# Gated delta rule in a two-layer trunk: keys read back and measured ahead of the gates, turned tiles stored in token order, one exponential for a chunk's decay

## The chip, the cores and the metric

The kernel runs on one core of a Trainium2 chip. The metric is the device time of one execution in microseconds, the median of several runs. TensorE (PE) multiplies matrices, VectorE (DVE), ScalarE (ACT) and GpSimd (POOL) work on tiles, and SyncE (SP) issues nearly all DMA transfers, in the order of its own queue. Each engine works through its instructions in the order in which the program holds them.

## The reference

Two layers run over 1024 tokens of width 1024. The change touches only the first layer's mixer. It projects the normed input to a gate branch (u, v), to q, k, v, to z and to two gate values per head, and runs a chunked delta rule on q, k, v:

```python
proj = rms_norm(h, ln_mix_e[i]) @ w_in_e[i]
a_uv, b_qkv, b_z, b_beta, b_a = jnp.split(proj, split_at, axis=-1)
qkv = jax.nn.silu(causal_depthwise_conv(qkv, conv_w))
q = l2_normalize(q) * (B_HEAD_DIM ** -0.5);  k = l2_normalize(k)
beta = jax.nn.sigmoid(beta_logit)
g = -jnp.exp(a_log) * jax.nn.softplus(a_logit + dt_bias)
gc = jnp.cumsum(g, axis=-1)                      # within a chunk
decay = exp(gc[t] - gc[s]) for s <= t, else 0
a = strict_lower((k * beta) @ k.T * decay);  t_mat = a + I
u = solve(t_mat, v * beta);  w = solve(t_mat, k * beta * exp(gc))
# one chunk after the other
v_new = u - w @ state
o = (q * exp(gc)) @ state + (q @ k.T * decay) @ v_new
state = state * exp(gc[-1]) + (k * exp(gc[-1] - gc)).T @ v_new
o = rms_norm(o, out_gain) * silu(z)
```

The layer goes on with an output projection, an MLP and a gated embedding; the second layer has attention instead of the mixer. All that is as it was.

## The kernel before, in words

The kernel keeps float32 accuracy by splitting every operand of a projection in a high and a low part, so that a product is three matmuls (`mm3`). The mixer works on 8 chunks of 128 tokens and 4 heads of 128. Its parts:

- **The fill.** `self.stream([...])` is a list of projections, cut in units. A unit of a `proj_qkv` is one step of the sum for 128 channels and 512 tokens: three matmuls of 512 columns. `pump(n)` emits units until n have been emitted in all. PE always has these units between the delta rule's own small matmuls, which are emitted at high priority and placed among them by a scheduler that writes each engine's order down. 256 units lie ahead of the first step of the recurrence. Weights are cast by ACT (L221) and DVE (L222).
- **A projected tile of q, k or v** is evicted by DVE (L1394), convolved by one ACT pass and three DVE passes (L1398, L1400), passed through tanh (L1402) and a product (L1407), turned in 32 by 32 blocks by DVE (`transpose`, L1408) into a temporary `t` and written to DRAM (`by_token`, L1409). The pool of `t` has four buffers; each tile takes two. `read_tokens` (L1365) brings one chunk back with tokens on the partitions: four transfers, each of 512 pieces of 128 bytes.
- **z** (`proj_z(0)`) also yields the gate values. `gates()` can start only when the last unit of `proj_z(0)` is done. It sums the gates within a chunk by PE (`pg`), turns the sums (`pgt`, L1335), copies them (L1337) and writes them to `g_dram` (L1338). `spatial_weights()` turns the gate branch's weights (`pws`).
- **`ahead(c)`**, for 8 chunks, reads the sums back on all partitions (`du`, L1602) and the chunk's keys as token rows (`kt`), forms the two decay masks `am` and `du` by eight exponentials of 128 columns (L1609) and two selections on POOL (L1610), measures the keys (`inverse_length`, L1582 to L1587), scales them (L1615), multiplies keys by keys on PE (`pkk`, into a PSUM pair shared with `pg`, `pgt`, `pws`), masks the product on DVE (L1629) and writes `am`, `du`, `kt` and the diagonal blocks of `am` to DRAM (L1591, L1632). `du` and `kt` have a place for each of four chunks (slots A0, A3), `am` has two (c6, d0).
- **`solve()`** reads the diagonal blocks of all chunks (L1641), inverts them on DVE in 30 steps of two instructions (L1647, L1648) and writes the result (`solved`, L1651). **`inverse(c)`** reads one chunk of it back (L1689, `inv`), turns it (L1693) and joins the blocks on PE (`py`, `pz`). **`step(c)`** is the recurrence (`pks`, `po`, `pvn`, `pst`), **`prep(c)`** readies its operands and reads v and q by `read_tokens`.

The order of emission is: `pump(96)`, `gates()`, `spatial_weights()`, `pump(104)`, the eight `ahead` spread over FILLA = 40 units, the solve over FILLB = 64, the first inverse over FILLC = 48, then chunk by chunk.

Of the kernel before, what the change touches and what calls it, by code (L numbers as in the profile page):

```python
# [11 lines left out]
F32 = mybir.dt.float32  # L12
# [6 lines left out]
P = 128  # L19
# [12 lines left out]
KA = (6, 5)  # L32
MARKS = ((64, 50), (192, 144), (223, 168))
TAIL = 220
FILLA, FILLB, FILLC = 40, 64, 48
IDLE = 5
FILLS = (24, 24, 24, 24, 28, 28, 28, 28)

# [76 lines left out]
class Trunk:  # L115
# [1141 lines left out]
    def even_mix(self, first, rows_of_rest, rest_of_x, w_in, ws, bs, conv, a_log, dt_bias, v_gain, o_gain, masks, w_out, gain_next, h_dram):  # L1257
# [81 lines left out]
            nc.vector.tensor_scalar(flat(nsum), pg[:, 0], -1.0, None, ALU.mult)  # L1339

        def spatial_weights():
            wsr = self.tmp().rearrange("p (g t) -> p g t", g=G)
            nc.sync.dma_start(wsr, ws.rearrange("g t s -> t g s"))
# [14 lines left out]
        def read_tokens(i, c, out):  # L1358

            hf, n = c // 4, c % 4  # L1360
            assert all((i, hf, m) in made for m in range(G))
            for j in range(4):
                z = slice(32 * j, 32 * j + 32)
                src = by_token[i, hf].rearrange("(a c) t -> c a t", c=32)[:, :, n * P + 32 * j : n * P + 32 * j + 32]
                nc.sync.dma_start(out[z].rearrange("c h (i r) -> c h i r", r=32), src.rearrange("c (h i) r -> c h i r", i=4))  # L1365

        def proj_qkv(i, j, hfs):

            def units(w):
                for hf in hfs:  # L1370
                    if (i, hf) not in by_token:
                        by_token[i, hf] = self.dp.tile([G * P, HT], F32, name=self.nm("by_token"))
                        if i < 2:
                            home(i, hf)

                    first = (i, hf, j) == (1, 0, 0)
                    pss = [self.mm_ps() for _ in range(2)] if first else []
                    for k, ml in itertools.product(range(KT), range(2)) if first else ():
                        self.mm3(pss[ml], w.at(k, slice(ml * P, (ml + 1) * P)), hs_first[k], k == 0, k == KT - 1)
                        if k < KT - 1:  # L1380
                            yield None
                    for ml in range(2):
                        m = i * 4 + j * 2 + ml
                        ps = pss[ml] if first else self.mm_ps()
# [12 lines left out]
                        y = self.tmp()  # L1397
                        nc.scalar.activation(y, cx[:, 3:], AF.Copy, scale=conv[:, 3, m : m + 1])  # L1398
                        for tap in range(3):
                            nc.vector.scalar_tensor_tensor(y, cx[:, tap : tap + HT], conv[:, tap, m : m + 1], y, ALU.mult, ALU.add)  # L1400
                        th = self.tmp()
                        nc.scalar.activation(th, y, AF.Tanh, scale=0.5)  # L1402
                        if i < 2:
                            y, y2 = qkv[i, hf][:, m % 4], y
                        else:
                            y2 = y
                        nc.vector.scalar_tensor_tensor(y, th, 1.0, y2, ALU.add, ALU.mult)  # L1407
                        nc.vector.transpose(th, y)  # L1408
                        nc.sync.dma_start(by_token[i, hf][(m % 4) * P : (m % 4 + 1) * P], th)  # L1409
                        made.add((i, hf, m % 4))  # L1410
                        yield None

# [168 lines left out]
        def inverse_length(pt, name, sq):  # L1581
# [4 lines left out]
            rn = self.sp.tile([P, G], F32, tag=name, name=self.nm(name), bufs=3)  # L1586
            nc.gpsimd.tensor_tensor(rn, l2, self.mhalf[:, 0:G], ALU.pow)  # L1587
            return rn

# [3 lines left out]
        def fetch(c, i, t):  # L1593
            nc.sync.dma_start(flat(t), spill[c, i])
            return t

        def ahead(c):

            if c == 0:
                early.extend(self.slot(t, [P, 4, HT], F32, "early") for t in ("A0", "A3"))  # L1600
            du, kt = (e[:, c % 4].rearrange("p (h t) -> p h t", h=G) for e in early)
            nc.sync.dma_start(flat(du), g_dram[G * c : G * c + G].rearrange("h t -> (h t)").partition_broadcast(P))  # L1602
            read_tokens(1, c, kt)
            yield
            yield
            am = self.slot(("c6", "d0")[c % 2], [P, G, P], F32, "dec")
            for e, own, other in ((am, gsum, 1), (du, nsum, -1)):
                for h in range(G):
                    nc.scalar.activation(e[:, h], du[:, h], AF.Exp, scale=-float(other), bias=own[:, c, h : h + 1])  # L1609
                nc.gpsimd.affine_select(e, e, pattern=[[0, G], [-other, P]], base=0, channel_multiplier=other, compare_op=ALU.is_gt if other > 0 else ALU.is_ge, fill=0.0)  # L1610
            keep(c, 1, du)

            k = part(1, c)
            rk = inverse_length(kt, "rk", self.slot(f"c{4 + c % 2}", [P, G, HD], F32, "sq"))
            nc.vector.tensor_tensor(kt, kt, bc(dec[:, c], HD), ALU.mult)  # L1615
# [12 lines left out]
            for h in range(G):  # L1628
                nc.vector.scalar_tensor_tensor(am[:, h], pp[:, h], sc[:, h : h + 1], am[:, h], ALU.mult, ALU.mult)  # L1629
# [21 lines left out]
            nc.sync.dma_start(solved, flat(x))  # L1651


        mid, ch, early = {}, {}, []

        def prep(c):
            kt = fetch(c, 2, self.slot(f"c{c % 2}", [P, G, HD], F32, "kt"))
# [129 lines left out]
        def mixing():  # L1787
# [15 lines left out]
        states = [state]  # L1803

        fill = itertools.chain(self.stream([
            proj_qkv(1, 0, (0,)), proj_qkv(2, 0, (0,)), proj_qkv(1, 1, (0, 1)), proj_z(0),
            proj_qkv(1, 0, (1,)), proj_qkv(2, 1, (0, 1)),
            proj_uv(1, 0), proj_uv(1, 1), proj_qkv(0, 0, (0,)), proj_qkv(0, 1, (0, 1)),
            proj_z(1), proj_qkv(0, 0, (1,)), proj_qkv(2, 0, (1,)), proj_uv(0, 0), proj_uv(0, 1)], first), mixing())
        closed = []  # L1810
# [12 lines left out]

        pump(2)
        self.wide = ("mm", "sc")
        rows_of_rest()
        for t, c in ((U, 0), (V, P), (mk, 2 * P)):
            nc.sync.dma_start(t, masks[:, c : c + t.shape[1]])
# [3 lines left out]
        nc.vector.tensor_scalar(og, og, 0.5, None, ALU.mult)  # L1832
        for _ in rest_of_x:
            pass
        pump(96)
        gates()
        spatial_weights()
        pump(104)


        def run(g, slot=True):
# [29 lines left out]
        self.pe.start(LAG)  # L1871
        solver = solve()
        systems = [ahead(c) for c in range(NC)]
        for i, n in enumerate(share(FILLA, NC + 3)):
            for j in range(min(i, NC - 1), max(0, i - 3) - 1, -1):
                run(systems[j], False)
            self.pe.slot()
            pump(done + n)
# [152 lines left out]
```

## Time and profile before

| | |
|---|---|
| median of 3 runs | 2528.28 us (2523.44 to 2531.18) |
| the profiled execution | 2529.31 us, its span 2527.6 us |
| PE busy | 2480.6 us, 98% of the span |
| DVE, ACT, POOL busy | 1867.0 us (74%), 1289.1 us (51%), 316.5 us (13%) |
| DMA | 457.76 MB, 59.9% of 16 engines; 239652 of 549876 packets under 512 bytes |

The span is cut in windows and chains by the profile; PE is busy nearly always, so a reader looks for the few stretches in which it is not. The mixer ahead of the recurrence lies in about the first 217 us.

### The profile page before, as it was taken

How to read it: one execution, taken by the hardware profiler on the slowest of the kernel's cores; microseconds unless marked ns; L12 is line 12 of the kernel's file. 1: busy time of each engine (PE TensorE's matmuls, PEld its weight loads, DVE VectorE, ACT ScalarE, POOL GpSimd, SP SyncE). 2: the span in 40 equal slices, each digit the busy share in tenths (PEclk: the TensorE clock that was granted, in tenths of full speed). 3: DMA queues.
4: the chain of work that ended last, by engine and by line, in shares of the span. 5: the costliest groups of instructions: out<-in, count | busy, mean ns of one | idle time of the engine just before them, and what ended most of it. 6: DMA issues, size and time to landing. Idle time of an engine off the chain costs nothing.

```text
span 2527.6 us, 39880 instructions
## 1 busy us (share of the span) xinstructions
PE 2480.6 (98%) x13599; PEld 2113.7 (84%) x13599; DVE 1867.0 (74%) x3611; ACT 1289.1 (51%) x2584; POOL 316.5 (13%) x280
## 2 busy tenths in 40 slices
PE   9979999999999999999999999999999999999999
PEld 7878898888888887888899999987788888878877
DVE  7777777687667779656568888885886677787586
ACT  6553444465455444454356766664655455445442
POOL 0220242000000000000234443341000000000000
PEclk9989999999999999999999999999999999999999
DMA  7584564547555855653347776799375558655651
GB/s 256 167 221 125 134 170 151 168 132 250 176 176 200 298 177 185 192 173 118 111 108 166 160 165 160 172 241 289 129 232 188 177 187 282 211 188 186 194 174 59
DMA packets 549876, 457.76 MB, mean 181 GB/s; under 512 B 239652, under 2 KB 412712, under 8 KB 549672
## 3 DMA queue, kind: packets, MB, share of 16 engines
q1 hardware_dynamic: 549656, 455.21, 59.9%
q8 instruction: 107, 1.75, 0.3%
q14 instruction: 97, 0.79, 0.1%
q10 hardware_dynamic: 16, 0.00, 0.0%
HBM read 320.86 MB, written 134.23 MB: 180 GB/s over the span
## 4 chain that ended last, share of the span: by engine, by line
PE 87%; DVE 4%; DMA 4%; SPq 2%; issue 1%; ACT 1%; POOL 0%; DVEq 0%; ACTq 0%; POOLq 0%
PE mm L76 77%; PE po L76 3%; PE qk L76 2%; PE aux L76 2%; SPq L1365 1%; PE tr L79 1%; DVE w L222 1%; DMA raw<-in_w_ple_gate_dram 1%; DMA aT<-a_dram 0%; DMA a_dram<-lg 0%; PE pgm L76 0%; DVE t L1400 0%; DVE acc L282 0%; DMA by_token<-t 0%; SPq L1632 0%
## 5 line engine op out<-in xcount | busy, mean ns | idle before, releaser
L76 PE MATMUL mm<-g,w 128*128 128x512 f32 x2592 | 603.8, 394 | 1.4 <-DVE acc L282 0.9
L221 ACT CAST w<-raw 128x512 fp32r<-128x512 f32 x598 | 364.7, 617 | 459.2 <-PE mm L76 376.0
L76 PEld LDWEIGHTS mm<-g,w 128*128 128x128 f32 x2592 | 485.9, 188 | 116.9 <-ACT w L221 1.3
L76 PE MATMUL mm<-hi,w 128*128 128x512 f32 x1728 | 555.4, 397 | 0.3 <-ACT hi L1248 0.3
L76 PE MATMUL mm<-w,hi 128*128 128x256 f32 (+2 forms) x2528 | 505.7, 296 | 3.3 <-ACT w L221 3.3
L222 DVE TENSOR_TENSOR w<-raw,w 128x512 fp32r<-128x512 f32 x510 | 353.2, 699 | 184.7 <-ACT w L221 178.7
L76 PEld LDWEIGHTS mm<-w,hi 128*128 128x128 f32 x2528 | 402.9, 190 | 17.6 <-ACT w L221 3.5
L76 PEld LDWEIGHTS mm<-hi,w 128*128 128x128 f32 x1728 | 325.8, 189 | 74.6 <-ACT hi L1248 0.7
L76 PE MATMUL mm<-w,lo 128*128 128x256 f32 (+2 forms) x1264 | 370.2, 294 | 0.0
L76 PE MATMUL mm<-lo,w 128*128 128x512 f32 x864 | 341.9, 396 | 0.9 <-DVE lo L1249 0.9
L76 PE MATMUL mm<-t,w 128*128 128x512 f32 x1152 | 270.8, 394 | 1.2 <-ACT w L221 1.2
L76 PEld LDWEIGHTS mm<-t,w 128*128 128x128 f32 x1152 | 216.2, 188 | 52.7 <-ACT w L221 1.6
L76 PEld LDWEIGHTS mm<-w,lo 128*128 128x128 f32 x1264 | 239.6, 190 | 6.1
L76 PEld LDWEIGHTS mm<-lo,w 128*128 128x128 f32 x864 | 163.4, 189 | 37.3 <-DVE lo L1249 1.4
L222 DVE TENSOR_TENSOR g<-graw,g 128x512 fp32r<-128x512 f32 x216 | 147.4, 686 | 10.6 <-DMA gd<-g 9.8
L221 ACT CAST g<-graw 128x512 fp32r<-128x512 f32 x216 | 132.7, 617 | 33.4 <-PE mm L76 10.8
L258 POOL TENSOR_TENSOR r<-ms,mhalf 128x4 f32<-128x4 f32 x12 | 13.3, 1108 | 1006.9 <-DVE ms L256 979.2
L1030 ACT ACTIVATE lg<-lg,nm 128x128 f32<-128x128 f32 (+7 forms) x128 | 99.2, 775 | 76.3 <-DVE nm L1027 75.5
L222 POOL TENSOR_TENSOR w<-raw,w 128x512 fp32r<-128x512 f32 (+1 forms) x88 | 114.9, 1326 | 142.7 <-ACT w L221 94.0
L348 ACT ACTIVATE g<-g 128x512 f32<-128x512 f32 x96 | 60.5, 632 | 120.5 <-DVE g L282 113.4
L1027 DVE CUSTOM_DVE_ANT_0 lg<-qk,al 128x512 f32<-128x512 f32 (+3 forms) x128 | 74.7, 587 | 27.6 <-PE qk L76 22.3
L76 PE MATMUL mm<-ohi,w 128*128 128x512 f32 x256 | 87.3, 406 | 1.4 <-DVE t L1207 1.4
(332 smaller groups left out, 3538.3 us busy)
## 6 DMA issues: line engine op xcount, KB each, us to landing
raw<-in_w_mlp_dram SPq DMA_DIRECT2D x352, 256.0 KB, 3.1
graw<-gd SPq DMA_DIRECT2D x224, 256.0 KB, 3.0
gd<-g SPq DMA_DIRECT2D x192, 256.0 KB, 3.2
raw<-in_w_ple_gate_dram SPq DMA_DIRECT2D x76, 256.0 KB, 3.2
acc<-h_dram SPq DMA_DIRECT2D x64, 256.0 KB, 4.4
keep<-in_w_mlp_dram SPq DMA_DIRECT2D x64, 256.0 KB, 4.9
raw<-in_w_in_e_dram SPq DMA_DIRECT2D x60, 256.0 KB, 3.9
h_dram<-acc SPq DMA_DIRECT2D x48, 256.0 KB, 2.3
```

Of the source, the lines that this page charges most:

```text
L76: self._next(self.engine.matmul(*a, **k))
L79: self._next(self.engine.transpose(*a, **k))
L221: self.nc.scalar.copy(hi, src)
L222: (lo_engine or self.nc.vector).tensor_tensor(lo, src, f32(hi), ALU.subtract)
L258: nc.gpsimd.tensor_tensor(r, ms, self.mhalf[:, 0:4], ALU.pow)
L348: nc.scalar.activation(g, src, AF.Relu)
L1027: nc.vector.tensor_tensor_reduce(out=lg[:, k0:k1], in0=ps[:, : k1 - k0], in1=al[:, u0 + k0 : u0 + k1], scale=-1.0, scalar=3.0e38 if c == 0 ...
L1030: nc.scalar.activation(lg[:, :n], lg[:, :n], AF.Exp, bias=nm[:, r, nch - 1 : nch], scale=-1.0, accum_out=me.sums[:, b, r : r + 1])
L1365: nc.sync.dma_start(out[z].rearrange("c h (i r) -> c h i r", r=32), src.rearrange("c (h i) r -> c h i r", i=4))
```

## The change

It has six parts.

1. The projections of keys for the second half of the tokens go ahead of `proj_z(0)`, so that all keys are projected before z. The gates then come after 112 units, not 96.
2. A turned tile is written in token order: four transfers of 32 partitions with 512 pieces of 128 bytes each (L1406). A chunk is read back by one transfer of whole rows (L1360).
3. A new generator `lengths(c)` reads and measures the keys of every chunk during the units of z, ahead of the gates. All 8 key tiles now have a place of their own (A0, A3).
4. `du` moves to two slots (c2, c3). POOL subtracts the sums from it once (L1610), and each mask is then one exponential of 512 columns (L1613).
5. The gate branch's weights are loaded near the start, to a slot of their own.
6. `ahead(c)` has three steps, not four; `pump(120)` precedes it, and FILLA, FILLB, FILLC become 36, 56, 44, so that 256 units still lie ahead of the recurrence.

```diff
-FILLA, FILLB, FILLC = 40, 64, 48
+FILLA, FILLB, FILLC = 36, 56, 44
...
-            for j in range(4):
-                z = slice(32 * j, 32 * j + 32)
-                src = by_token[i, hf].rearrange("(a c) t -> c a t", c=32)[:, :, n * P + 32 * j : n * P + 32 * j + 32]
-                nc.sync.dma_start(out[z].rearrange("c h (i r) -> c h i r", r=32), src.rearrange("c (h i) r -> c h i r", i=4))
+            nc.sync.dma_start(flat(out), by_token[i, hf][n * P : (n + 1) * P])
...
-                        nc.sync.dma_start(by_token[i, hf][(m % 4) * P : (m % 4 + 1) * P], th)
+                        for a in range(4):
+                            f0 = (m % 4) * P + 32 * a
+                            nc.sync.dma_start(by_token[i, hf].rearrange("(t c) f -> c t f", c=32)[:, :, f0 : f0 + 32], th[32 * a : 32 * a + 32].rearrange("c (t r) -> c t r", r=32))
...
+        def lengths(c):
+            if c % 4 == 0:
+                early.append(self.slot(("A0", "A3")[c // 4], [P, 4, HT], F32, "early"))
+            kt = early[c // 4][:, c % 4].rearrange("p (h d) -> p h d", h=G)
             read_tokens(1, c, kt)
             yield
+            rks.append(inverse_length(kt, "rk", self.slot(f"c{4 + c % 2}", [P, G, HD], F32, "sq"), NC))
...
+            du = self.slot(f"c{2 + c % 2}", [P, G, P], F32, "dec")
+            nc.sync.dma_start(flat(du), g_dram[G * c : G * c + G].rearrange("h t -> (h t)").partition_broadcast(P))
+            yield
+            nc.gpsimd.tensor_tensor(du, du, bc(gsum[:, c], P), ALU.subtract)
...
-            for e, own, other in ((am, gsum, 1), (du, nsum, -1)):
-                for h in range(G):
-                    nc.scalar.activation(e[:, h], du[:, h], AF.Exp, scale=-float(other), bias=own[:, c, h : h + 1])
+            for e, other in ((am, 1), (du, -1)):
+                nc.scalar.activation(flat(e), flat(du), AF.Exp, scale=-float(other))
...
-            proj_qkv(1, 0, (0,)), proj_qkv(2, 0, (0,)), proj_qkv(1, 1, (0, 1)), proj_z(0),
-            proj_qkv(1, 0, (1,)), proj_qkv(2, 1, (0, 1)),
+            proj_qkv(1, 0, (0,)), proj_qkv(2, 0, (0,)), proj_qkv(1, 1, (0, 1)), proj_qkv(1, 0, (1,)),
+            proj_z(0), proj_qkv(2, 1, (0, 1)),
...
+        wsr = self.slot("c8", [P, G, P], F32, "wsr")
+        nc.sync.dma_start(wsr, ws.rearrange("g t s -> t g s"))
...
-        pump(96)
+        pump(80)
+        tokens = [lengths(c) for c in range(NC)]
+        for i in range(NC + 1):
+            if i:
+                next(tokens[i - 1])
+            if i < NC:
+                next(tokens[i])
+            pump(done + (i < NC) * 4)
         gates()
         spatial_weights()
-        pump(104)
+        pump(120)
...
-        for i, n in enumerate(share(FILLA, NC + 3)):
-            for j in range(min(i, NC - 1), max(0, i - 3) - 1, -1):
+        for i, n in enumerate(share(FILLA, NC + 2)):
+            for j in range(min(i, NC - 1), max(0, i - 2) - 1, -1):
```

In the lists below, numbers after a name tell buffers of the same name apart, and x4 is four equal instructions. The first place is PE where the gates' sums are turned (`pgt`) and the keys' products begin (`pkk`). Before:

```order
L76 MATMUL mm_1371<-hi_127,w_1099 128x512
L79 MATMUL pgt_1079<-ident,carved_239 32x128
L76 MATMUL mm_1371<-lo_128,w_1099 128x512
L76 MATMUL mm_1371<-hi_127,w_1100 128x512
L76 MATMUL mm_1371<-hi_136,w_1099 128x512
L76 MATMUL mm_1371<-lo_137,w_1099 128x512
L76 MATMUL mm_1371<-hi_136,w_1100 128x512
L79 MATMUL pws_1087<-ident,t_1085 128x128
L76 MATMUL pkk_1280<-qkv_275 128x128 x4
L79 MATMUL pws_1087<-ident,t_1085 128x128 x3
```

and now, where `wsr` holds the gate branch's weights:

```order
L76 MATMUL mm_1434<-hi_554,w_1107 128x512
L79 MATMUL pgt_1277<-ident,carved_239 32x128
L79 MATMUL pws_1283<-ident,wsr_288 128x128 x4
L76 MATMUL pkk_1399<-qkv_275 128x128 x4
L76 MATMUL mm_1434<-hi_605,w_1188 128x512
L76 MATMUL mm_1434<-lo_606,w_1188 128x512
L76 MATMUL mm_1434<-hi_605,w_1189 128x512
```

`pgt` stands 41 matmuls of 512 columns later in PE's order than before. Behind it the second `pkk` comes after 12 matmuls of the fill (15 before) and the third after 9 more (12 before). The first `py` stands 27 rows later than before, nearly all of them matmuls of 512 columns.

The second place is SP's queue from the write of the gates' sums on, where `early_1143` and `dec` hold decays and `dec_1194`, `dec_1254` are `am` of the first two chunks. Before:

```order
L1338 DMA g_dram<-t_1081 32x128
L1602 DMA early_1143<-g_dram 128x512 x4
L1409 DMA by_token_702<-t_1138 128x512
L1632 DMA diag<-dec_1194 32x4x32
L1591 DMA spill<-early_1143 128x512
L1632 DMA diag<-dec_1194 32x4x32 x2
L1591 DMA spill<-early_1143 128x512
L1632 DMA diag<-dec_1194 32x4x32
L1591 DMA spill<-dec_1194 128x512
L1602 DMA early_1143<-g_dram 128x512
```

and now, where `dec_1337`, `dec_1355`, `dec_1383`, `dec_1447` are `du` of chunks 0 to 3 and `dec_1358`, `dec_1386` are `am` of chunks 0 and 1:

```order
L1338 DMA g_dram<-t_1279 32x128
L1608 DMA dec_1337<-g_dram 128x512
L1608 DMA dec_1355<-g_dram 128x512
L1406 DMA by_token_437<-t_1329 32x16x32 x4
L101 DMA raw_2128<-in_w_in_e_dram 128x2x256
L1588 DMA spill<-dec_1337 128x512
L1636 DMA diag<-dec_1358 32x4x32
L1588 DMA spill<-dec_1355 128x512
L1636 DMA diag<-dec_1358 32x4x32 x2
L1608 DMA dec_1383<-g_dram 128x512
L1636 DMA diag<-dec_1358 32x4x32
```

Four reads of the sums stood together; now two do, and the third is queued behind the write of the first chunk's `du`, whose slot it takes. POOL's order has the same pairs: subtractions of chunks 2n and 2n+1, then four selections.

The third place is ACT at the last four chunks, where `dec_1557`, `dec_1596`, `dec_1664` are `am` of chunks 4, 5, 6, `t_1761` and `t_1845` are GELU tiles of the gate branch, and `qkv_2300` is v of the first four chunks. Before (ACT's last exponentials and what followed):

```order
L1609 ACTIVATE early_1143<-early_1143,carved_239 128x128
L1609 ACTIVATE dec_1636<-early_1143,carved_239 128x128 x4
L1609 ACTIVATE early_1143<-early_1143,carved_239 128x128 x4
L1476 ACT_TABLE_LOAD
L1476 ACTIVATE t_1806<-mm_1745,r_217 128x256 x2
```

and now:

```order
L1473 ACTIVATE t_1761<-mm_1648,r_217 128x256 x2
L1613 ACT_TABLE_LOAD
L1613 ACTIVATE dec_1557<-dec_1489 128x512
L1613 ACTIVATE dec_1489<-dec_1489 128x512
L1613 ACTIVATE dec_1596<-dec_1554 128x512
L1613 ACTIVATE dec_1554<-dec_1554 128x512
L1673 ACTIVATE qkv_2300<-qkv_2300,carved_240 128x128 x16
L1613 ACTIVATE dec_1664<-dec_1593 128x512
L1473 ACT_TABLE_LOAD
L1473 ACTIVATE t_1845<-mm_1779,r_217 128x256 x2
L1613 ACT_TABLE_LOAD
```

GELU tiles now stand among the exponentials, with five table loads from the first GELU to the end of the masks where there was one, and v is scaled (16 passes) before the masks of the last two chunks.

More of the change, by code (lines that the diff above doesn't have):

```diff
@@ L1341, in spatial_weights @@
         def spatial_weights():
-            wsr = self.tmp().rearrange("p (g t) -> p g t", g=G)
-            nc.sync.dma_start(wsr, ws.rearrange("g t s -> t g s"))
             pt = aux([P, G, P], "aux", "pws")
@@ L1371, in units @@
                     if (i, hf) not in by_token:
-                        by_token[i, hf] = self.dp.tile([G * P, HT], F32, name=self.nm("by_token"))
+                        by_token[i, hf] = self.dp.tile([4 * P, G * HD], F32, name=self.nm("by_token"))
                         if i < 2:
@@ L1579, in part, with inverse_length @@
             return qkv[i, hf][:, :, slice((c % 4) * P, (c % 4 + 1) * P)]
-        def inverse_length(pt, name, sq):
+        def inverse_length(pt, name, sq, bufs=3):
             nc.scalar.activation(sq, pt, AF.Square)
@@ L1585, in inverse_length @@
             nc.vector.tensor_scalar(l2, l2, 4 * EPS, None, ALU.add)
-            rn = self.sp.tile([P, G], F32, tag=name, name=self.nm(name), bufs=3)
+            rn = self.sp.tile([P, G], F32, tag=name, name=self.nm(name), bufs=bufs)
             nc.gpsimd.tensor_tensor(rn, l2, self.mhalf[:, 0:G], ALU.pow)
@@ L1595, in fetch, with ahead @@
             return t
[L1597 to L1602, printed above, removed]
+        early, rks = [], []
+        def lengths(c):
+            if c % 4 == 0:
+                early.append(self.slot(("A0", "A3")[c // 4], [P, 4, HT], F32, "early"))
+            kt = early[c // 4][:, c % 4].rearrange("p (h d) -> p h d", h=G)
             read_tokens(1, c, kt)
             yield
+            rks.append(inverse_length(kt, "rk", self.slot(f"c{4 + c % 2}", [P, G, HD], F32, "sq"), NC))
             yield
+        def ahead(c):
+            du = self.slot(f"c{2 + c % 2}", [P, G, P], F32, "dec")
+            nc.sync.dma_start(flat(du), g_dram[G * c : G * c + G].rearrange("h t -> (h t)").partition_broadcast(P))
+            yield
+            nc.gpsimd.tensor_tensor(du, du, bc(gsum[:, c], P), ALU.subtract)
             am = self.slot(("c6", "d0")[c % 2], [P, G, P], F32, "dec")
-            for e, own, other in ((am, gsum, 1), (du, nsum, -1)):
-                for h in range(G):
-                    nc.scalar.activation(e[:, h], du[:, h], AF.Exp, scale=-float(other), bias=own[:, c, h : h + 1])
+            for e, other in ((am, 1), (du, -1)):
+                nc.scalar.activation(flat(e), flat(du), AF.Exp, scale=-float(other))
                 nc.gpsimd.affine_select(e, e, pattern=[[0, G], [-other, P]], base=0, channel_multiplier=other, compare_op=ALU.is_gt if other > 0 else ALU.is_ge, fill=0.0)
@@ L1613, in ahead @@
             k = part(1, c)
-            rk = inverse_length(kt, "rk", self.slot(f"c{4 + c % 2}", [P, G, HD], F32, "sq"))
+            kt, rk = early[c // 4][:, c % 4].rearrange("p (h d) -> p h d", h=G), rks[c]
             nc.vector.tensor_tensor(kt, kt, bc(dec[:, c], HD), ALU.mult)
@@ L1651, in solve @@
             nc.sync.dma_start(solved, flat(x))
-        mid, ch, early = {}, {}, []
+        mid, ch = {}, {}
         def prep(c):
```

## The prediction

> **What bounds the kernel now.** I read the page first, then the windows of the mixer, then what PE waited for there, then the timelines of the engines that released it. The page:
>
> ```profile
> span 2527.6 us, 39880 instructions
> PE 2480.6 (98%) x13599; PEld 2113.7 (84%) x13599; DVE 1867.0 (74%) x3611; ACT 1289.1 (51%) x2584; POOL 316.5 (13%) x280
> ```
>
> PE is the bound, so an edit gains only where PE stands idle or runs at a throttled clock. Windows of 20 us (columns: PE, PEld, DVE, ACT, POOL busy, granted clock, DMA share, GB/s) and PE's waits from 100 to 215 us:
>
> ```profile
> 100.00:120.00 20.00, 14.89 (x71) 12.48 (x70) 15.20 (x43) 7.28 (x20) 4.41 (x5) 0.83 0.67 216
> 120.00:140.00 20.00, 15.10 (x71) 12.21 (x69) 16.39 (x37) 10.60 (x26) 3.29 (x5) 0.91 0.80 199
> 140.00:160.00 20.00, 13.06 (x92) 13.06 (x93) 15.83 (x51) 12.86 (x38) 10.11 (x14) 0.74 0.77 230
> 160.00:180.00 20.00, 16.69 (x138) 16.49 (x138) 6.98 (x24) 8.77 (x24) 0.32 (x1) 0.98 0.86 208
> ...
> PE pkk L76 <- DVE dec L1629: 11.8, 2, 10.0
> PE pws L79 <- DMA t<-in_gmlp_ws_dram: 5.1, 1, 5.1
> PE mm L76 <- ACT w L221: 3.3, 1, 3.3
> ```
>
> Exactly these three waits, 20.2 us, are the idle time of the four windows (5.1 + 4.9 + 6.9 + 3.3). Behind them the clock drops. Narrow windows:
>
> ```profile
> 109.80:113.00 3.20, 3.19 (x14) 3.10 (x15) 0.36 (x1) 0.72 (x1) 0.00 (x0) 0.50 0.61 158
> 128.00:131.50 3.50, 3.50 (x14) 3.08 (x14) 3.50 (x8) 0.99 (x4) 1.51 (x2) 0.52 0.82 279
> 146.90:152.00 5.10, 5.06 (x24) 5.06 (x25) 3.99 (x13) 1.48 (x3) 1.36 (x3) 0.51 0.88 296
> 179.00:185.00 6.00, 6.00 (x40) 6.00 (x39) 5.54 (x14) 3.44 (x9) 0.00 (x0) 0.72 0.99 297
> ```
>
> Their loss is 1.6 + 1.7 + 2.5 + 1.7 = 7.5 us. So at most about 28 us lie open here; the change aims at all of it. But behind the waits runs a chain that PE does not see until `py` needs the inverse. Its landmarks (PE, DVE, SP; start, duration):
>
> ```profile
> 103.28 0.27 PE L79 MATMUL pgt<-ident,carved 128*32 128x128 f32 x1
> 104.73 0.27 DVE L1337 COPY t<-pgt 32x128 f32<-32x128 f32 x1
> 105.55 0.49 SPq L1338 DMA_DIRECT2D g_dram<-t  x1
> 109.86 1.76 SPq L1602 DMA_DIRECT2D early<-g_dram  x4
> 115.84 1.12 DVE L1629 SCALAR_TENSOR_TENSOR dec<-pkk,sc,dec 128x128 f32<-128x128 f32 x4
> 159.24 1.13 DVE L1629 SCALAR_TENSOR_TENSOR dec<-pkk,sc,dec 128x128 f32<-128x128 f32 x4 [1.24 <-POOL dec L1610]
> 171.18 0.21 DVE L1647 TENSOR_TENSOR outer<-work 128x30 f32<-128x30 f32 x1 [3.04 <-DMA work<-diag]
> 196.96 0.19 DVE L1648 TENSOR_TENSOR work<-work,outer 128x30 f32<-128x30 f32 x1
> 207.18 0.31 DVE L1693 STREAM_TRANSPOSE inv<-inv 128x128 f32<-128x128 f32 x1 [4.16 <-DMA inv<-solved]
> 210.98 0.44 PE L76 MATMUL py<-inv,am 32*32 32x32 f32 x16
> ```
>
> From the write of the gates' sums (105.55) to the turned inverse (207.5) the chain takes 102 us; PE comes to `py` at 210.98, 3.5 us later and without a wait. The chain has hardly any slack, and that decides this change.
>
> **The change, step by step.** *The gates come later.* PE reaches `pgt` 41 matmuls of 512 columns later. Three of them take 97.94 - 97.24 = 0.70 us:
>
> ```profile
> 97.24 0.63 PE L76 MATMUL mm<-hi,w 128*128 128x512 f32 x2
> 97.94 0.63 PE L76 MATMUL mm<-hi,w 128*128 128x512 f32 x2
> ```
>
> So PE alone puts `pgt` 9.5 us later, at 112.8. Ahead of the copy L1337 DVE now has two more convolved tiles, four more reductions and four more scalings:
>
> ```profile
> L1400 DVE SCALAR_TENSOR_TENSOR t<-cx,cols,t 128x512 f32<-128x512 f32 x31 | 24.4, 786 | 0.8 <-ACT t L1398 0.6
> L1615 DVE TENSOR_TENSOR early<-early,carved 128x512 f32<-128x512 f32 x8 | 5.4, 682 | 0.0
> ```
>
> Six taps at 0.79 and fourteen others at about 0.69 (all read 512 columns, as L1615 does) are 14.4 us, some 13 us with the overlap of neighbours. If DVE were full, the copy would come at 117.9; by PE alone at 113.1. Walking DVE's order behind the last gate values (it waits for the two table loads of the gates, as before, then has eight scalings in a row) I take 116.3: the sums are written at 116.6, **11.0 us later** (8 to 12.6).
>
> *The wait for `pws` goes* (5.1 us), but what it hid comes out: the third `pkk` needs the first product masked, and PE has only `pws`, two `pkk` and 21 matmuls, some 7 us, to cover the round trip of the sums.
>
> *The decay ring.* `du` had four places and now has two. A pair of chunks must be read, subtracted, selected and written out before the next pair's read may start:
>
> ```profile
> L1509 POOL TENSOR_TENSOR guv<-guv,mean 128x512 f32<-128x512 f32 x8 | 8.2, 1040 | 17.2 <-DVE mean L1508 17.2
> L1445 POOL TENSOR_TENSOR z<-z,carved 128x512 f32<-128x512 f32 x4 | 6.4, 1595 | 55.2 <-DVE z L1444 55.2
> L1610 POOL TENSOR_SCALAR_AFFINE_SELECT dec<-dec 128x512 f32<-128x512 f32 x8 | 5.3, 658 | 21.4 <-ACT dec L1609 15.7 <-DMA diag<-dec 5.7
> L1609 ACT ACTIVATE dec<-early,carved 128x128 f32<-128x128 f32 x32 | 10.1, 389 | 14.5 <-DMA spill<-dec 11.8 <-DMA early<-g_dram 2.7
> ```
>
> The landing times, from the answers on the lines L1602 (read of sums), L1591 (write of a decay tile), L1632 (128-byte writes) and L1365 (128-byte reads), in this order:
>
> ```profile
> DMA to landing us min/median/max: 3.4/4.0/5.2
> DMA to landing us min/median/max: 2.1/3.0/4.0
> DMA to landing us min/median/max: 1.4/2.3/4.2
> DMA to landing us min/median/max: 1.9/2.5/6.5
> ```
>
> The subtraction is not in this trace; L1509 has its very form, a row of four values taken from 512 columns (1.04), L1445 is the dear end (1.60). A pair then costs 4.0 (read) + 1.04 x 2 (POOL has the partner's subtraction ahead of the selections, partly in the partner's reading time) + 0.66 x 2 + 3.0 (write) + 0.4 (issue) = 10.8 us. The exponentials become cheaper (one pass of 512 columns in place of four of 128 at 0.39 each), but they lie in the shadow of POOL; I take nothing for them. First read at 116.6 + 4.3 = 120.9; the fourth pair's read three rings later, and 1.9 us more because its slots wait behind GELU and table loads: 155.2. Then landing and subtraction, and on ACT two table loads and a GELU ahead of the last mask, then selection and product: 11.9 us. The last product ends at **167**, 50.5 us after the sums; before it ended at 160.4, 54.8 after them. The removed reads of keys (the 10.0 us wait) are thus nearly spent on the ring. From there to the solve, five issues, the landing and the two reads: 11.5 us as before (159.24 + 1.13 to 171.18 is 10.8): the solve starts at 178.6.
>
> Table loads, the place where a page speaks:
>
> ```profile
> 91.05 1.28 ACT L1324 ACT_TABLE_LOAD   x1
> 92.34 0.32 ACT L1324 ACTIVATE carved<-carved,ones 128x32 f32<-128x32 f32 x1
> ```
>
> I use 1.28, since the next pass starts 1.29 us after the load. The Trainium skill, "ScalarE: Activation LUTs", section "What ACT_TABLE_LOAD costs", adds a drain to the load, about 2.66 us for each switch; by it the two loads in the chain would cost 2.8 us more and my sum would be 2532.1. The row shows no such drain.
>
> *The solve.* It took 26.0 us with four weight splits (L222) inside. By the order, eight splits, two evictions and three taps now stand inside, nine instructions more. Three are taps at 0.79, six are like L1615 (0.68) or smaller: at most 6.5 us, and I take 3.7, since DVE now also waits in the solve's pauses that they would fill: 29.7, and it ends at 208.3.
>
> *Back to PE.* 10.0 us before (197.15 to 207.18). Now SP has three writes of a turned q tile ahead of the reads of `inv`, where it had two weight loads: 9.5. `py` is at **217.8**. Before, it was at 210.98; but 27 matmuls more are done by then (6.3 us). Net 0.5 us late. PE itself would arrive near 208.5, for it loses some 20 us on the way (at the third, fifth and seventh `pkk`, and to the clock) instead of 28. So it idles about 9 us at `py`, a new place, and 2.0 us of clock follow (between the 1.7 and 2.5 above).
>
> *Reads of v and q* (L1360) are one transfer, not four; SP saves 12 us around 165 (16 issues), off PE's path except for the 3.3 us wait, whose end is covered by the wait at `py` now. Later:
>
> ```profile
> 164.92 11.98 SPq L1365 DMA_DIRECT2D qkv<-by_token  x16
> PE pks L76 <- DVE qkv L1765: 1.1, 1, 1.1
> PE po L76 <- DVE dec L1676: 0.8, 1, 0.8
> ```
>
> The two waits in the recurrence follow reads of v by such a queue; I take 1.5 us of their 1.9 (0 to 4 with clock).
>
> *Writes of turned tiles*: three more issues each, about 1.5 us of SP for 24 tiles, in stretches where SP has gaps. They hold a buffer `t` for about 0.7 (transpose) + 4 x 0.49 (issues, as L1338) + 2.5 (landing) = 5.2 us; the tile after next needs it some 9 us after the transpose by the timeline. Nothing on the path. The early weight load is one issue: nothing.
>
> **The sum:** +0.5 + 2.0 - 1.5 = +1.0 us. The profiled run took 2529.31 us with a span of 2527.6, 1.0 above the median of 2528.28. Forecast: a span of 2528.6, a median of **2529.3**.
>
> **The rivals.** *A: the chain keeps ahead of PE, faster.* Writes land at 2.1 and reads at 3.4 (their minima, since SP and the DMA queues carry fewer small reads), so a ring takes 9.3 us: -4.5. The gates' copy is not held by DVE: -3.2. The wait at `py` shrinks from 9 to about 1.5 us, so the clock loss goes too: -2. Together -9.7: 2519.6. For it: the trace's landings are those of a crowded stretch (DMA share 0.67 to 0.88). Against it: all three are at their ends. Faster by over 0.3% (7.6 us, about what a measurement of this kernel can tell from no change) means below 2520.7. Chance 0.24.
>
> *B: the ring runs at the dear end, slower.* Reads land at 5.2, writes at 4.0, and POOL subtracts at 1.60 while DVE works: 10.8 becomes 14.1, three rings make +9.9, all of it at `py`, which is on the path: 2539.2. It decides from 13 us a ring on (three times 2.2 above mine: 2535.9). For it: L1445 next to a busy DVE. Against it: the medians. Chance 0.23.
>
> *C: token-order writes are slow.* If pieces of 128 bytes, four transfers in a row, landed later than about 6.6 us, the tanh two tiles on would wait for its buffer; at 8 us that is 1.4 us on each of the eight tiles ahead of the gates that reuse one: +11, 2540. Against it: L1632 writes such pieces in 2.3, no later than L1365 reads them. The Trainium skill, "DMA: Bandwidth & Descriptors", section "Specifications", says that below 512 B a transfer does read-modify-write; by it the change moves the small pieces to the dear side. Chance 0.07.
>
> **How the numbers follow.** The forecast's own range is 2521 to 2536 (the write of the sums 3 us earlier or 1.6 later, a ring 1.5 us cheaper or 2.2 dearer), chance 0.46. A has 0.24, B and C 0.30. The range of eight in ten reaches from A's middle region to B's and C's: 2515 to 2544. Faster 0.24, same 0.46, slower 0.30.
>
> **What would show it.** Right: PE waits for `pkk` at the third, fifth and seventh, none for `pws` or for ACT w near 175, and one of 6 to 12 us at `py` near 208 to 218; the reads L1608 come in pairs 10 to 12 us apart; DVE's solve starts at 175 to 182. Wrong: no wait at `py` (A); pairs 13 us apart or more (B); L1406 landing at over 6 us and DVE or ACT waiting for it before 100 us (C); or new waits in the recurrence after 220, which I have not costed.

## The result, and the profile after

The changed kernel takes 2529.22 us (median of 12 runs, 2526.06 to 2533.11) against 2527.34 us for the kernel before in the same runs: a ratio of 1.0009, interval 1.0000 to 1.0018. The profiled execution took 2532.61 us, 3.4 above its own median; that of before, 2529.31, was 2.0 above.

The page of the changed kernel, PE's waits in its first 480 us, and one window over the mixer for both kernels, before first (columns as in the windows of the prediction):

```profile
span 2530.9 us, 39823 instructions
```

```profile
PE pkk L76 <- DVE dec L1633: 9.4, 3, 4.6
PE pgt L79 <- DVE carved L1333: 7.4, 1, 7.4
PE py L76 <- DVE inv L1697: 2.0, 1, 2.0
...
PE po L76 <- DVE qkv L1745: 1.6, 1, 1.6
PE pkq L76 <- DVE qkv L1402: 1.6, 1, 1.6
```

```profile
100.00:240.00 140.00, 119.74 (x762) 106.85 (x761) 101.19 (x258) 58.63 (x143) 18.52 (x25) 0.91 0.63 175
```

```profile
100.00:240.00 140.00, 116.99 (x725) 103.61 (x725) 92.58 (x240) 55.29 (x99) 28.41 (x33) 0.88 0.59 169
```

The waits for `pws` and for a cast weight are gone, as the change means them to be. A wait of 7.4 us at `pgt` and three around the start of the recurrence (5.2 together: `po`, `pkq` and, last, `py`) stand in their place. PE is idle 23.0 us in this window, 20.3 before, and its granted clock is lower, 0.88 against 0.91. The chain behind it, at the places that the prediction followed (PE, DVE, SP; start, duration):

```profile
104.23 0.97 PE L76 MATMUL pg<-carved,carved 128*128 128x32 f32 x8
118.72 0.17 DVE L1333 COPY carved<-pg 128x32 f32<-128x32 f32 x1
118.95 0.39 PE L79 MATMUL pgt<-ident,carved 128*32 128x128 f32 x1 [7.39 <-DVE carved L1333]
120.85 0.27 DVE L1337 COPY t<-pgt 32x128 f32<-32x128 f32 x1
121.15 0.86 SPq L1338 DMA_DIRECT2D g_dram<-t  x1
125.59 0.80 SPq L1608 DMA_DIRECT2D dec<-g_dram  x2
135.94 0.38 SPq L1608 DMA_DIRECT2D dec<-g_dram  x1
146.29 0.55 SPq L1608 DMA_DIRECT2D dec<-g_dram  x1
160.51 0.34 SPq L1608 DMA_DIRECT2D dec<-g_dram  x1
171.41 1.13 DVE L1633 SCALAR_TENSOR_TENSOR dec<-pkk,sc,dec 128x128 f32<-128x128 f32 x4 [3.06 <-POOL dec L1614]
183.88 0.21 DVE L1651 TENSOR_TENSOR outer<-work 128x30 f32<-128x30 f32 x1 [1.28 <-DMA work<-diag]
212.55 0.18 DVE L1652 TENSOR_TENSOR work<-work,outer 128x30 f32<-128x30 f32 x1
221.70 0.64 PE L76 MATMUL py<-inv,am 32*32 32x32 f32 x16 [1.98 <-DVE inv L1697]
```

From the write of the sums to the last masked product 51.4 us (171.41 + 1.13 less 121.15), to the solve 11.3, through it 28.9, back to `py` 9.0. All this is near the forecast. The sums themselves are late, and `py` comes at 221.70, 3.9 us behind the forecast of 217.8. Why L1333 comes only at 118.72, although PE had made its input (`pg`) by 105.2, the timelines of ACT and DVE tell:

```profile
106.66 0.63 ACT L1579 ACTIVATE sq<-early 128x512 f32<-128x512 f32 x1 [4.39 <-DMA early<-by_token]
110.59 0.23 ACT L1332 ACTIVATE carved<-pg 128x96 f32<-128x96 f32 x1
```

```profile
107.33 0.69 DVE L1581 TENSOR_REDUCE l<-sq 128x4 f32<-128x512 f32 x1 [3.81 <-ACT sq L1579]
113.23 0.68 DVE L1619 TENSOR_TENSOR early<-early,carved 128x512 f32<-128x512 f32 x1
```

The measuring of the last keys stands ahead of the gates on both engines and waits for its DMA read; then seven scalings of keys go ahead of the copy, which PE's `pgt` waits for.

The mark used below for the end of the mixer is the first time that PE turns the recurrence's last tiles (`pab` of `qkv`). These are its rows and the windows up to it, before first:

```profile
466.23 0.60 PE L79 MATMUL pab<-ident,qkv 128*128 128x128 f32 x4
470.84 0.60 PE L79 MATMUL pab<-ident,qkv 128*128 128x128 f32 x4
```

```profile
0.00:466.23 466.23, 437.48 (x3089) 389.20 (x3090) 344.75 (x797) 212.47 (x468) 98.04 (x101) 0.97 0.60 174
0.00:470.84 470.84, 441.17 (x3089) 391.26 (x3090) 345.44 (x797) 210.18 (x424) 103.66 (x109) 0.96 0.60 173
```

The mark lies 4.6 us later. PE did the same 3089 matmuls up to it; 3.7 us of the difference is busy time and 0.9 idle time.

### The profile page after: what moved, and what is told of

The parts are those of the page before. It is cut to its first block, busy times and chain, and to the rows that moved or that the text cites. A ratio compares the mean times of both kernels' runs of the same rounds, so it can differ in the third digit from the quotient of the medians.

```text
span 2530.9 us, 39823 instructions
## 1 busy us (share of the span) xinstructions
PE 2482.3 (98%) x13599; PEld 2115.2 (84%) x13599; DVE 1867.5 (74%) x3611; ACT 1288.1 (51%) x2540; POOL 322.5 (13%) x288
## 4 chain that ended last, share of the span: by engine, by line
PE 86%; DMA 5%; DVE 5%; issue 2%; SPq 1%; ACT 1%; POOL 0%; DVEq 0%; POOLq 0%; ACTq 0%
PE mm L76 76%; PE po L76 3%; PE aux L76 2%; PE qk L76 2%; DMA aT<-a_dram 1%; PE tr L79 1%; DMA raw<-in_w_mlp_dram 1%; DVE w L222 0%; DVE t L1395 0%; DMA by_token<-t 0%; DVE outer L1651 0%; DVE work L1652 0%; DMA spill<-dec 0%; PE pgm L76 0%; DVE lg L1027 0%
## 5 line engine op out<-in xcount | busy, mean ns | idle before, releaser
L222 DVE TENSOR_TENSOR w<-raw,w 128x512 fp32r<-128x512 f32 (+1 forms) x510 | 349.8, 693 | 177.8 <-ACT w L221 171.5
L221 ACT CAST g<-graw 128x512 fp32r<-128x512 f32 x216 | 132.7, 617 | 31.7 <-PE mm L76 10.4
```

The costliest lines, as they stand in the source:

```text
L221: self.nc.scalar.copy(hi, src)
L222: (lo_engine or self.nc.vector).tensor_tensor(lo, src, f32(hi), ALU.subtract)
```

## The experiments

Two theories stood against each other. **W**: the sums are late because their copy is queued on DVE behind the keys. **R**: the two places of the decays pace the chain whatever the gates do. The scheduler writes a new order for every kernel, so a run differs from its neighbour in more than its edit; where a trace shows that this mattered, the text says so.

**Gates first.** The changed kernel with

```diff
-            nc.vector.tensor_tensor(kt, kt, bc(dec[:, c], HD), ALU.mult)
+            self.pe.behind(nc.vector.tensor_tensor(kt, kt, bc(dec[:, c], HD), ALU.mult), marks["sums"])
...
-        gates()
+        with self.tc.high_priority(EARLY):
+            gates()
...
```

and, by the same `behind`, the squares and reductions of chunks 4 to 7, which are now emitted after the gates.

> The changed kernel, with the gates emitted at high priority and, on DVE and ACT, the squares and reductions of chunks 4 to 7 and all eight scalings of keys put behind the copy of the turned sums (by order of issue only). Theory W (the sums are late because their copy stands in DVE's queue behind the measuring of keys): the copy of the sums (118.72 in the changed kernel) comes at 104 to 108, PE's wait of 7.4 us at pgt goes, the sums are written at 112 to 114 instead of 121.15, the last masked product ends at 163 to 166 instead of 172.5, py comes 6 to 9 us earlier, time 2520 to 2523, ratio to before 0.996 to 0.998. Theory R (the two places of the decays pace the chain whatever the gates do): the wait at pgt goes, but the waits at pkk grow from 9.4 us to 15 or more and the time stays at 2527 to 2530.

2526.48 us, ratio 0.9997 (0.9987 to 1.0007). The wait at `pgt` went, the sums were written at 113.50, 7.65 us earlier. PE's waits behind them (100 to 240 us), and the first and last steps of the solve:

```profile
PE pkk L76 <- DVE dec L1639: 13.1, 3, 5.8
PE py L76 <- DVE inv L1703: 5.0, 1, 5.0
```

```profile
178.60 0.21 DVE L1657 TENSOR_TENSOR outer<-work 128x30 f32<-128x30 f32 x1 [1.48 <-DMA work<-diag]
212.57 0.18 DVE L1658 TENSOR_TENSOR work<-work,outer 128x30 f32<-128x30 f32 x1
```

The waits moved: 3.7 us more at `pkk`, 3.0 more at `py`. The solve starts 5.3 us earlier, but now has 27 instructions of other work (14.5 us) in it on DVE, 16 (9.9 us) in the changed kernel; it takes 34.1 us instead of 28.9 and ends at the same moment, 212.7, and `py` is only 1.8 earlier. W explains the wait at `pgt`, not the time. R comes closer without being met in full (it expected 15 us or more at `pkk` and 2527 to 2530). How much of the gain went to the two places and how much to the new order within the solve, this run does not separate.

**Four places for the decays.**

```diff
-            du = self.slot(f"c{2 + c % 2}", [P, G, P], F32, "dec")
+            du = self.slot(("c2", "c3", "c0", "c1")[c % 4], [P, G, P], F32, "dec")
```

> The changed kernel, with the decays on four places (c2, c3, c0, c1) instead of two. Theory R (the ring of two places paces the chain, 10.35, 10.35 and 14.2 us a pair): the first four reads of the sums go out together at about 125, PE's waits at pkk shrink from 9.4 to under 5 us, the last masked product ends at 164 to 168 instead of 172.5, py waits under 2 us, time 2522 to 2525. Rival M (the two places of am and POOL pace it as much): the reads go out early, the last masked product ends within 2 us of 172.5, time 2527 to 2530. Theory W expects that the wait of 7.4 us at pgt stays in either case.

2526.98 us, ratio 0.9996 (0.9987 to 1.0005). Four reads left together at 124.87; the last masked product ended at 169.6, 2.9 us earlier, between the two expectations; the time is at the edge of rival M's range.

```profile
PE pkk L76 <- DVE dec L1633: 8.2, 4, 2.8
PE pgt L79 <- DVE carved L1333: 7.3, 1, 7.3
```

The late sums remain. Behind them the third chunk's mask starts on ACT at 140.57, behind the write of a decay tile, though its sums were subtracted by 134.1, and the last pair's masks stand on ACT behind v and GELU, at 165.87. So the two places of `am` are likely what holds the third chunk, but not the last pair; no run gave `am` more places. R alone is not the answer either.

**Both**, run twice.

> Both edits together: gates first and four places. If W and R are both right and each holds its own part: 2514 to 2519. If they cover one another, as two waits of the same chain: no more than 2 us better than the better of the two alone. If only M holds: as with the gates first alone.

> The third run's kernel once more, unchanged, beside the three that follow, since they are compared with it and five of its runs counted: 2517 to 2521, ratio to before 0.995 to 0.9975.

2519.10 us, ratio 0.9960 (0.9947 to 0.9972), and again 2517.62 us, 0.9960 (0.9947 to 0.9973). Alone the two edits are worth 2 to 3 us of the changed kernel's 2529.22, hardly more than their intervals tell from nothing, together 10 to 12. The mark, of one execution each, tells the same: 470.84 in the changed kernel, 467.81 and 468.50 with one edit, 459.54 and 460.42 with both. They are two links of one chain: with either left in, the chain is still late, and most of the other's gain turns into a wait. Part of what remained in the second of these runs, on PE, SP and ACT:

```profile
PE mm L76 <- ACT t L1475: 4.3, 1, 4.3
```

```profile
168.33 7.79 SPq L1408 DMA_DIRECT2D by_token<-t  x9
```

```profile
174.55 1.28 ACT L1475 ACT_TABLE_LOAD   x1 [7.20 <-DMA by_token<-t]
```

Nine issues of token-order writes stand on SP behind transfers of the last masked product; they hold temporaries, GELU (L1475) waits for one, and PE for GELU. PE's idle time between 100 and 240 us is 18.5 us here.

**The parts of the change alone, in the kernel before.** First the early weights (`wsr` loaded at the start to c8, nothing else):

> The kernel before, with one part of the change alone: the gate branch's weights are loaded at the start to a slot of their own. Theory of moved waits (the one the prediction used): the wait of 5.1 us at pws goes, PE reaches the later pkk earlier and waits there longer, 15 to 18 us instead of 11.8, and the time is within 0.1% of before (2525 to 2529). Rival: the wait is a plain loss and its end is a plain gain, 5.1 us and about 1.5 us of clock: 2520 to 2522.

2523.22 us, ratio 0.9981 (0.9972 to 0.9990): 4.2 us gained. The wait for `pws` went and two others grew (11.8 and 3.3 before):

```profile
PE pkk L76 <- DVE dec L1627: 17.1, 3, 13.0
PE mm L76 <- ACT w L221: 5.6, 1, 5.6
```

Idle time between 100 and 240 us even grew, from 20.3 to 22.7 at the same mean clock of 0.91. So the theory of moved waits is right on the waits. The mark still came 2.1 us earlier, at 464.09 instead of 466.23, as PE waited 2.2 us less from 240 to 500. Neither expectation holds in full, and where the rest of the 4.2 us comes from stays open.

Then one exponential (POOL subtracts, decays keep four places):

```diff
-            for e, own, other in ((am, gsum, 1), (du, nsum, -1)):
-                for h in range(G):
-                    nc.scalar.activation(e[:, h], du[:, h], AF.Exp, scale=-float(other), bias=own[:, c, h : h + 1])
+            nc.gpsimd.tensor_tensor(du, du, bc(gsum[:, c], P), ALU.subtract)
+            for e, other in ((am, 1), (du, -1)):
+                nc.scalar.activation(e, du, AF.Exp, scale=-float(other))
```

> The kernel before, with one part of the change alone: POOL subtracts the sums once, each mask is one exponential of 512 columns; the decays keep their four places. Theory P (the exponentials lie in POOL's shadow, the subtraction adds 1.04 us a chunk to the chain): PE's wait for masked products stays at 11 to 16 us, time 2526 to 2531. Rival: ACT's passes did pace the chain (12.9 us busy in 140 to 160), and it gets shorter: the wait shrinks to 6 to 9 us, time 2521 to 2525.

2530.78 us, ratio 1.0018 (1.0009 to 1.0026): 4.1 us lost, within theory P's range; the wait for masked products is 13.8 us in two, one of 13.1, 2.0 more than before. That is a third of the 5.9 us by which PE's idle time from 100 to 240 us grew: a new wait of 2.4 us for an evicted tile and 1.3 more for a cast weight are most of the rest. That the subtraction on POOL costs the time is thus not shown.

Then token order alone:

> The kernel before, with one part of the change alone: turned tiles written in token order by four transfers, a chunk read back by one. Theory P (as in the prediction: the writes are hidden, the reads take fewer issues): PE's wait of 11.8 us for masked products shrinks to 5 to 9, the wait of 3.3 us for a cast weight goes, time 2519 to 2524. Rival C (token-order writes land late and hold the temporaries): landings above 6 us, DVE and ACT wait for them before 100 us, time 2530 to 2540.

2534.27 us, ratio 1.0032 (1.0022 to 1.0043): 7.6 us lost. Its profiled execution, 2529.0, was the fastest of its ten and no slower than the profiled one of before (2529.31), and its mark (468.71) is only 2.5 us later, so the trace can show only a part of that loss. PE's wait, and SP where the last keys are written and read back; behind them SP of the kernel before:

```profile
PE pkk L76 <- DVE dec L1628: 19.9, 2, 18.1
```

```profile
125.72 0.91 SPq L1408 DMA_DIRECT2D by_token<-t  x2
135.92 0.34 SPq L1601 DMA_DIRECT2D early<-g_dram  x1
136.30 2.06 SPq L1408 DMA_DIRECT2D by_token<-t  x4
140.26 1.76 SPq L1362 DMA_DIRECT2D early<-by_token  x4
```

```profile
125.88 0.32 SPq L1409 DMA_DIRECT2D by_token<-t  x1
130.98 4.02 SPq L1365 DMA_DIRECT2D early<-by_token  x8
```

Theory P fails. Rival C's time is met, but not its mechanism: the writes land fast (2.1 us in the median). A tile's write is four entries of SP's queue now, and for the last tile of keys two of them stand behind a read that waits for its place until 135.92. The first of these keys are read 9.3 us later, and PE's long wait goes from 10.0 to 18.1. In this trace the order of the queue did that, and not the landing of small pieces; where the rest of the 7.6 us lies stays open.

**Token order in the new arrangement.** "Both" with the old transfers (one write a tile, four reads of a chunk):

> Gates first and four places, as in the third run, with the token order taken back: one write a tile, four reads of 128-byte pieces a chunk. If the one-issue reads carry part of the gain: 2 to 6 us slower than the third run, 2521 to 2525, with the reads of keys late. If the four writes a tile cost more than the reads save (ACT waited 7.45 us for a write of a turned tile there, and PE 4.5 us behind it): the wait of 4.5 us goes and the time is 2514 to 2518.

2534.24 us, ratio 1.0028 (1.0017 to 1.0039), 15 to 17 us slower than "both", where 2 to 6 was expected. PE's longest wait, and SP:

```profile
PE mm L76 <- ACT t L1476: 10.3, 1, 10.3
```

```profile
108.26 8.87 SPq L1365 DMA_DIRECT2D early<-by_token  x16
177.82 7.55 SPq L1365 DMA_DIRECT2D qkv<-by_token  x9
```

Sixteen reads of keys occupy SP until 117.1, and the write of the sums behind them comes at 117.76, 5.1 us later than in "both". The last of sixteen reads of v keep SP until 185.4; ACT waits for them with GELU queued behind. So in this arrangement token order is worth more than the two edits of "both". The run takes writes and reads back together; the two rows point at the reads, but no run has one without the other.

**Places of their own for turned tiles.** "Both", and

```diff
+                        if done >= 64 and (2, 1) not in qkv:
+                            if not stage:
+                                stage.append(self.slot("A5", [P, 4, HT], F32, "stage"))
+                            th = stage[0][:, len(made) % 4]
                         nc.vector.transpose(th, y)
```

> Gates first and four places, as in the third run; the turned tiles go through four places of their own (A5, free until v of the second half) instead of the temporaries. Theory T (token-order writes, queued on SP behind work that waits for the last masked product, hold the temporaries that GELU needs): ACT's wait of 7.45 us for a write of a turned tile and PE's wait of 4.5 us behind it go, time 2513 to 2517. Rival: GELU then waits for its own writes to uv_dram or PE waits as long at py, time 2518 to 2521.

2512.17 us, ratio 0.9939 (0.9922 to 0.9956), the fastest of all: 14.7 us below the kernel before, 5 to 7 below "both". The wait behind GELU is gone; the largest wait of PE that is left, and its window:

```profile
PE pkk L76 <- DVE dec L1643: 6.3, 2, 4.5
```

```profile
100.00:240.00 140.00, 128.25 (x872) 114.52 (x871) 112.04 (x283) 60.23 (x115) 32.31 (x37) 0.96 0.70 193
```

Against the second run of "both" idle time fell from 18.5 to 11.8 us, of which 4.3 is the wait behind GELU, and the clock rose from 0.95 to 0.96. The solve is shorter too, 24.3 us against 31.7, with 6 instructions of other work in it and not 10; what the places are worth without that order is not separated.

**The sums turned earlier**, on "both" and on the places of their own: `self.pe.floor = first_sums` after unit 115, so that `pgt` comes 12 matmuls earlier.

> Gates first and four places, as in the third run, and PE turns the sums 12 matmuls earlier (the fill behind unit 115 comes behind it in PE's order), right behind the copy that it needs. Theory W: the sums are written at 108 to 109.5 instead of 112.6, the wait of 4.6 us at the third pkk shrinks to under 1.5, the solve ends 2 to 4 us earlier, time 2514 to 2517. Rival M (the two places of am pace the chain behind it): the third pkk's wait shrinks, but the later waits of PE up to 180 grow by as much; 2518 to 2520.

> The same places of their own, with PE turning the sums 12 matmuls earlier as in the seventh run (2523.6). Theory T: its wait of 8.4 us behind GELU goes, and what the earlier turn gained shows: 2511 to 2516. Rival: the wait is not the temporaries' and stays, 2520 to 2524.

2523.59 us, 0.9985 (0.9976 to 0.9994), and 2520.30 us, 0.9968 (0.9956 to 0.9980): both slower than without. In the first the sums were written at 108.23 as expected, but PE then waited 8.4 us behind GELU. In the second that wait was gone, as theory T has it, and yet the time was the rival's. In its trace 26 instructions of other work (14.3 us) stood in the solve on DVE, where the run before had 6 (3.6 us): its last step stands at 205.30 instead of 197.50, and PE waited for it. The mark is 4.9 us later, 458.45 against 453.57. The last steps, the run before first, and PE's wait:

```profile
197.50 0.19 DVE L1662 TENSOR_TENSOR work<-work,outer 128x30 f32<-128x30 f32 x1
205.30 0.17 DVE L1662 TENSOR_TENSOR work<-work,outer 128x30 f32<-128x30 f32 x1
```

```profile
PE py L76 <- DVE inv L1707: 4.5, 1, 4.5
```

**Four exponentials again**, on "both":

> Gates first and four places, as in the third run, with the exponentials taken back: eight passes of 128 columns a chunk with the sums as bias, nothing subtracted on POOL. Theory P (one exponential puts 1.04 us of POOL into each chunk's chain and costs, 4.1 us in the sixth run): 2 to 5 us faster than the third run, 2513 to 2517. Rival (here ACT is the fuller engine, and the passes stand among GELU and table loads): 2 to 4 us slower, 2521 to 2524.

2519.77 us, ratio 0.9974 (0.9962 to 0.9986), against 0.9960 (0.9947 to 0.9973): not told apart, and outside both expectations. The one exponential, which came with a loss of 4.1 us in the order before, neither costs nor gains anything measurable here.

## Why the prediction was right, and where it was not

The number was right: forecast 2529.3 within 0.3% of before, measured 2529.22. Its way was right in part, and the agreement is in part luck. Of the signs that it named, PE's waits at the third, fifth and seventh `pkk` came, and none for `pws` or a cast weight; two pairs of reads came 10.35 us apart, the third 14.2; but `py` waited 2.0 us, not 6 to 12, and the solve started at 183.88, not by 182.

- **The gates come later: mis-sized.** Forecast: sums written at 116.6, 11.0 us later, 12.6 at most. Measured: 121.15, 15.6 later. The step counted DVE's work ahead of the copy, not that DVE stands still for 3.8 us behind ACT and a read, nor that `pgt` needs L1333 from the same queue. PE's wait of 7.4 us at `pgt` is a term that the sum lacked. Of these 4.6 us beyond the forecast 3.9 are still there at `py`.
- **The ring: right in sum.** 10.35, 10.35 and 14.2 us for three pairs, 34.9 in all; forecast 3 x 10.8 + 1.9 = 34.3. POOL's subtraction took 1.04 us in the median, as its nearest row had it, and 1.59 at most.
- **Solve and the way back: right.** 11.3, 28.9 and 9.0 us; forecast 11.5, 29.7 and 9.5.
- **The wait at `py`: the size was off.** The forecast had nine in one; 2.0 came at `py` and 3.2 in two waits just ahead of it, at `po` and `pkq`, since PE had already lost 7.4 at `pgt`.
- **The clock: mis-sized.** Forecast 2.0 us behind `py`, and less than before ahead of it. The narrow windows behind the waits:

```profile
118.90:126.00 7.10, 6.10 (x21) 5.02 (x22) 6.24 (x18) 1.24 (x2) 3.03 (x4) 0.52 0.64 223
133.40:139.10 5.70, 5.68 (x17) 4.85 (x18) 5.10 (x14) 2.01 (x5) 0.90 (x1) 0.50 0.54 185
144.70:149.00 4.30, 4.23 (x36) 4.23 (x37) 4.30 (x14) 0.00 (x0) 1.10 (x2) 1.00 0.56 147
157.00:163.00 6.00, 5.93 (x28) 5.93 (x29) 1.54 (x8) 4.78 (x16) 0.61 (x2) 0.50 0.80 232
221.70:228.50 6.80, 6.80 (x31) 5.42 (x32) 2.16 (x7) 1.24 (x3) 0.00 (x0) 0.53 0.18 31
```

Busy time times the missing clock is 2.9 + 2.8 + 3.0 + 3.2 = 11.9 us, against 7.5 before.

- **Reads of v: right in sum, by luck.** The waits from 280 to 480 us fell by 1.7 us; forecast 1.5. But 1.1 of it is a wait for a split operand (`alo`), which the forecast did not name; of the two waits that it named (1.9) one of 0.7 is left and a new one, for the state, grew by 0.6.
- **Table loads.** In the changed kernel a load of 1.28 us is followed by its pass after 1.29 (150.34 and 151.63), so the 2.66 us with a drain of the Trainium skill, "ScalarE: Activation LUTs", section "What ACT_TABLE_LOAD costs", did not show.
- **Writes at nothing: not so once the chain is shorter.** In the changed kernel no wait of PE ends with such a write, though GELU waits 9.1 us for one. Token order alone, writes and reads together, lost 7.6 us. In "both" a write of a turned tile held GELU and PE 4.3 us behind it, and places of their own gained 5 to 7 us. They are not rival C: L1406 landed in 2.3 us in the median (1.7 to 4.3), the whole-tile write of before in 2.5, so the read-modify-write below 512 B of the Trainium skill, "DMA: Bandwidth & Descriptors", section "Specifications", does not show as a later landing.
- **The early load at nothing:** one issue, but alone it gains 4.2 us.

Up to the mark the forecast had +1.0 us, and the profiled execution shows +4.6 (0.9 of idle time, 3.7 of busy time for the same matmuls). From there to the end it was 1.3 us shorter than that of before, which the forecast did not have; the spans differ by 3.3, the medians by 1.9. So the sum was 3.6 us too low for the execution that it was made against. Single executions of the changed kernel differ by more than that (2526.06 to 2533.11), and the difference of the medians has an interval of 0 to 4.5 us, so the agreement of the medians to 0.1 us is luck.

Rival A falls with the late sums, B with the ring (11.6 us a pair in the mean, where it needs 13), C with the landings. No run moved the order of the projections without the rest of the change. The difference between the whole (+1.9) and the three parts run alone (-4.2, +4.1, +7.6) would make it worth about 5.6 us with its reads; but by the mark (+4.6 against -2.1, +2.9, +2.5) it would cost 1.3. The parts do not add, as the runs on "both" show, and not even the sign of this one is shown.

## What to carry to other kernels

When two links of a chain are late, an experiment that mends one may show almost nothing: look where its gain went and mend both before a verdict. A transfer that is split in four is four entries of an in-order queue: look at what a program's order puts between them, and which buffer waits for the last. An instruction on the path is as late as the slowest wait ahead of it in its engine's queue, so a copy that PE waits for belongs ahead of work that waits for memory.

## What was not expected of the hardware

The granted clock fell to 0.50 to 0.53 behind waits of 3.2, 4.6 and 7.4 us and behind three waits of 1.6 to 2.0 us within 8 us, for 5.7 to 7 us each time; behind a single wait of 1.62 us (144.77) it stayed at 1.00, while one of 1.82 in the kernel before was followed by 0.52. The Trainium skill, "TensorE: Matmul & The Clock Gate", section "Part 1: The HAM clock gate", puts the drop behind an idle window of about 3.4 us; here the wait of 1.82 us and the three short ones were enough. What sets the two cases of 1.62 and 1.82 apart, no run here shows.
